# Key-query products of a delta-rule scan by row halves, with loads two steps ahead

## The chip, the core and the metric

The kernel runs on one core of one Trainium2 chip. The metric is the time of one execution on the device, in microseconds; lower is better. Engines are named as the profile names them: PE multiplies matrices (PEld is its loading of the stationary operand), DVE, ACT and POOL work on vectors, and SP issues most of the transfers.

## What is computed

The reference is a two-layer backbone over 512 latent and 256 context tokens. Layer 1 mixes time with a bidirectional RWKV-7 recurrence, and only its scan is touched here:

```python
def wkv_scan(r, w, kk, bvec, k, v, s0, reverse):
    def step(s, inp):
        r_t, w_t, kk_t, b_t, k_t, v_t = inp
        sk = jnp.einsum('bhvk,bhk->bhv', s, kk_t)
        s = s * w_t[:, :, None, :] - sk[..., None] * b_t[:, :, None, :] + v_t[..., None] * k_t[:, :, None, :]
        return s, jnp.einsum('bhvk,bhk->bhv', s, r_t)
```

The delta rule is the term with `sk`: each token takes from the state what the state says under its key `kk_t`. The scan runs over the context first, then over the latent tokens, once forwards and once backwards, for 16 heads of 64 columns.

## The kernel before

The scan works on chunks of 64 tokens. `order` (line 1049) pairs a forward chunk with a backward one: 4 steps over the context, then 8 over the latent tokens, 12 in all. A step handles both directions `d` and, for each of 8 values of `kt`, two heads `n`. On the 128 partitions, direction 0 has its keys and queries in rows 64 to 127 and direction 1 in rows 0 to 63 (`half(1 - d)`).

Two functions share the work. `tm_step(i, kt)` carries the recurrence of step `i` for one pair of heads: products into the PSUM tile `sc` (line 47 is the helper that issues every matmul), with ACT, DVE and POOL between them. `tm_feed(i + 1)` is a generator that prepares the next step; `tm_scan` advances it once after each `kt` of step `i`. It issues the loads of the keys (`KB`, line 1067), queries (`QZ`, line 1068) and values (`W`, line 1071), then forms the products of keys and queries in four groups `g`, masks them into `G` (DVE, line 1082), copies the raw queries into half of `G` (ACT, line 1089), and transposes the keys (line 1096).

The product of one head is one matmul for both directions:

```python
x = 2 * m * (2 * j + n)
self.mm(ps[:, x:x + 2 * m], KB[g // 2][:, 2 * (g % 2) + j, n], QZ[:, 2 * g + j, n, :, 0:m], True, True)
```

The stationary operand is `KB`, 128 rows by 128 columns. `QZ` holds the two directions side by side, and the rows of the other direction are zeros, set once by POOL (line 1289). A context step has `m` = 64 (the delta rule's queries alone), a latent step `m` = 128 (these, and the output's queries behind them). In fp32 every matmul appears in the profile as two passes, each with a load of its stationary operand. `tm_step` reads the output's queries from `QZ` too, for the product `sc<-S,QZ`.

The buffers decide when a load may start: `KB` has 2 buffers, both of one step; `QZ` has 2, one for each step; `W` has 2. So the keys of the next step wait for the transposes of this feed, and its queries for the last read of the step before.

The order on each engine is not the order of the code: a scheduler with a timing model sets it when the program is built, and each engine then runs its list strictly in order. Transfers are SP's list. `tm_invert` and `tm_below` (the inverses of the triangular blocks) and `tm_post` (normalisation of finished chunks) run in between, on DVE, POOL, ACT and PE.

Of the kernel before, what the change touches and what calls it, by code (L numbers as in the profile page):

```python
# [7 lines left out]
F32 = mybir.dt.float32  # L8
F32R = mybir.dt.float32r
I32 = mybir.dt.int32  # L10
AF = mybir.ActivationFunctionType
# [4 lines left out]
P = 128  # L16
D = 1024
KT = 8
# [16 lines left out]
class Net:  # L35
# [908 lines left out]
    def tm_prep(self, kt, lw):  # L944
# [49 lines left out]
        for d in range(2):  # L994
# [4 lines left out]
            else:  # L999
                (nc.vector if kt == KT - 1 else nc.gpsimd).tensor_mul(X[:, 1], X[:, 1], k)  # L1000
                ek, eq, er = E[1][:, :, 0:64], E[0][:, :, 1:65], E[0][:, :, 0:64]
            nc.gpsimd.tensor_copy(self.dec0[:, kt, d], E[1][:, :, 64])
            KB = self.sb([P, 12, 128], F32, "KB", 3)
            nc.vector.tensor_mul(KB.rearrange("p c (b i) -> p b c i", b=2), X.rearrange("p b (c i) -> p b c i", i=64),
                                 ek.unsqueeze(1).to_broadcast([P, 2, 12, 64]))
            nc.sync.dma_start(self.kbd[d, kt], KB)
            ql, qc = self.sb([P, 8, 128], F32, "ql", 3), self.sb([P, 4, 64], F32, "qc", 3)
# [41 lines left out]
    order = [(c, 19 - c) for c in range(8, 12)] + [(c, 7 - c) for c in range(8)]  # L1049
    half = staticmethod(lambda n: slice(64 * n, 64 * n + 64))  # L1050

    def tm_feed(self, i, KB=None, W=None):

        nc, half = self.nc, self.half
        f = self.feeds[i] = {}
        cs = self.order[i]
        lat = cs[0] < 8
        m = 128 if lat else 64
        KB = KB or [self.sb([P, 4, 2, 128], F32, "KB", 2) for _ in range(2)]
        W = f["W"] = W or self.sb([P, KT, 2, 2, 64], F32, "W", 2)  # L1060
        QZ = f["QZ"] = self.QZ[i % 2]
        by = lambda z: z.rearrange("k (n p) m -> p (k n) m", n=2)
        flat = lambda z: z.rearrange("p k n m -> p (k n) m")
        for d in range(2):
            h = half(1 - d)
            for g in range(2):
                nc.sync.dma_start(flat(KB[g][h]), by(self.kbd[d, 4 * g:4 * g + 4, :, cs[d]]))
            nc.sync.dma_start(flat(QZ[h, :, :, d, 0:m]), by(self.qld[d, :, :, cs[d]] if lat else self.qcd[d, :, :, cs[d] - 8]))
        for d in range(2):
            v = self.vd[64 * cs[d]:64 * cs[d] + 64].rearrange("t (k n v) -> t k n v", n=2, v=64)  # L1070
            nc.sync.dma_start(W[half(d), :, d], v)
        f["G"], f["KT"] = [], []
        yield
        for g in range(4):
            ps = self.mm2()
            for j in range(2):
                for n in range(2):
                    x = 2 * m * (2 * j + n)
                    self.mm(ps[:, x:x + 2 * m], KB[g // 2][:, 2 * (g % 2) + j, n], QZ[:, 2 * g + j, n, :, 0:m], True, True)
            G = self.sb([P, 2, 2, 2, m], F32, "G", 8)  # L1080
            f["G"].append(G)
            nc.vector.tensor_mul(G.rearrange("p k n d t -> p (k n) d t"),  # L1082
                                 ps[:, :8 * m].rearrange("p (k d t) -> p k d t", d=2, t=m),
                                 self.gmask[:, :, 0:m].unsqueeze(1).to_broadcast([P, 4, 2, m]))
            if i:

                for d in range(2):
                    h = half(1 - d)
                    nc.scalar.activation(G[h, :, :, d, 0:64], QZ[h, 2 * g:2 * g + 2, :, d, 0:64], AF.Copy)
            yield  # L1090
        for g in range(2):
            ps = self.mm2()
            for j in range(4):
                for n in range(2):
                    x = 256 * j + 128 * n
                    nc.tensor.transpose(ps[:, x:x + 128], KB[g][:, j, n], self.ident)  # L1096
            T = self.sb([P, 4, 2, 128], F32, "KT", 3, pool=self.gp)
            nc.scalar.activation(T, ps.rearrange("p (k n x) -> p k n x", k=4, n=2), AF.Copy)
            f["KT"].append(T)
            yield  # L1100
# [58 lines left out]
    def tm_step(self, i, kt):  # L1159

        nc, half, order = self.nc, self.half, self.order
        f, cs = self.feeds[i], order[i]
        lat, first, last = cs[0] < 8, i == 0, i == len(order) - 1
        g, j = kt // 4, kt % 4
        W = f["W"][:, kt]
        XT = self.XT[i // 2][:, i % 2]
        Q = f["QZ"][:, kt]
        G = f["G"][kt // 2][:, kt % 2]
        K = f["KT"][g][:, j]
        S, Sd = self.S[g], self.Sd[g]  # L1170
        units = [(d, n) for n in range(2) for d in range(2)]
        pr = self.ps([P, 512], "sc", 4, pool=self.sps)
        col = lambda b, d: slice(128 * b + 64 * d, 128 * b + 64 * d + 64)
        for d, n in units:
            h = half(d) if first else slice(0, P)
            self.mm(pr[half(1 - d), col(0, n)], G[h, n, d, 0:64], W[h, d, n], True, True)
        rh = self.sb([P, 2, 64], F32, "rh", 4, pool=self.gp)
        nc.scalar.activation(rh, pr[:, 0:128].rearrange("p (n v) -> p n v", n=2), AF.Copy)
        for d, n in units:
            h = half(1 - d)  # L1180
            self.mm(pr[h, col(1, n)], XT[h, n, kt], rh[h, n], True, True)
        nc.vector.copy_predicated(W, self.umask.unsqueeze(2).unsqueeze(3).to_broadcast([P, 2, 2, 64]),
                                  pr[:, 128:256].rearrange("p (n v) -> p n v", n=2).unsqueeze(1).to_broadcast([P, 2, 2, 64]))
        if not last:
            for d, n in units:
                self.mm(pr[half(1 - d), col(2, n)], K[:, n, half(1 - d)], W[:, d, n], True, True)
            if j == 0:
                self.S2 = self.sb([P, 4, 2, 64], F32, "S", 4, pool=self.gp)
            for n in range(2):
                m = self.dec[:, n, kt, i:i + 1]  # L1190
                if first:
                    nc.vector.tensor_scalar(self.S2[:, j, n], pr[:, col(2, n)], m, None, op0=OP.mult)
                else:
                    nc.vector.scalar_tensor_tensor(self.S2[:, j, n], pr[:, col(2, n)], m, Sd[:, j, n],  # L1194
                                                   op0=OP.mult, op1=OP.add)
            if j == 3:
                W2 = self.feeds[i + 1]["W"]
                for d in range(2):
                    h = half(1 - d)
                    nc.scalar.activation(W2[h, 4 * g:4 * g + 4, d], self.S2[h], AF.Copy)  # L1200
            if j == 3 and i < len(order) - 2:
                m = self.dec[:, :, 4 * g:4 * g + 4, i + 1].rearrange("p n k -> p k n")
                self.Sd[g] = self.sb([P, 4, 2, 64], F32, "Sd", 3, pool=self.gp)
                nc.gpsimd.tensor_mul(self.Sd[g], self.S2, m.unsqueeze(3).to_broadcast([P, 4, 2, 64]))
        if lat:
            units = [(d, n) for d in range(2) for n in range(2)]
            for d, n in units:
                self.mm(pr[half(n), col(3, d)], G[:, n, d, 64:128], W[:, d, n], d == 0, False)
            for d, n in units:
                self.mm(pr[half(n), col(3, d)], Q[:, n, d, 64:128], S[:, j, n], False, d == 1)  # L1210
            lo, hi = min(cs), max(cs)
            Y = self.Y[:, kt, lo:hi + 1:hi - lo]
            o = pr[:, 384:512].rearrange("p (d v) -> p d v", d=2)
            if cs[0] < cs[1]:
                nc.scalar.activation(Y, o, AF.Copy)
            else:
                nc.vector.tensor_add(Y, Y, o[:, ::-1])
        if j == 3 and not last:
            self.S[g] = self.S2
# [56 lines left out]
    def tm_scan(self):  # L1276
        nc, a, half = self.nc, self.a, self.half
# [1 line left out]
        nc.sync.dma_start(self.gmask, a["gmask"])  # L1279
        self.umask = self.sb([P, 2], I32, "umask")  # L1280
        nc.sync.dma_start(self.umask, a["umask"])

        qz = lambda j: self.sb([P, KT, 2, 2, 128], F32, "QZ%d" % j)
        q = qz(0)
        ahead = [self.sb([P, 4, 2, 128], F32, "KB", 2) for _ in range(2)], self.sb([P, KT, 2, 2, 64], F32, "W", 2)
        self.QZ = [q, qz(1)]
        for j, z in enumerate(self.QZ):
            for d in range(2):
                nc.gpsimd.memset(z[half(d), :, :, d], 0.0)  # L1289
        self.feeds, self.S, self.Sd = {}, [None, None], [None, None]  # L1290
        n, below = len(self.order), iter(())
        for _ in self.tm_feed(0, *ahead):
            pass
        for i in range(n):
            feed = self.tm_feed(i + 1) if i + 1 < n else iter(())
            for kt in range(KT):
                self.tm_step(i, kt)
# [230 lines left out]
```

## Time and profile before

| | |
|---|---|
| median of 3 runs | 2260.74 us (2259.57 to 2262.29) |
| the profiled execution | 2269.31 us, 0.38% over the median |
| its span | 2267.5 us |
| PE busy in the span | 2023.4 us (89%) |
| DVE, ACT, POOL busy | 1145.4, 869.6, 519.6 us |
| mean granted clock of PE | 0.942 |
| the scan, by its first and last product | about 1464 to 1815 us of the span |

The span is the time from the first to the last instruction of the profiled execution. PEclk is the granted share of PE's full clock of 2.4 GHz; 0.5 is 1.2 GHz. A busy share is an average over stages: outside the scan PE is busy nearly all of the time, inside it is not.

### The profile page before, as it was taken

To read this page: it belongs to the slowest core of one execution; us is meant where nothing else is said; L and a number is where in the kernel's file an instruction comes from. 1 tells how busy PE (TensorE), PEld (TensorE's weight loads), DVE (VectorE), ACT (ScalarE), POOL (GpSimd) and SP (SyncE) were. 2 spreads that over 40 slices of the span, in tenths; PEclk is the share of its full clock that TensorE was granted. 3 is DMA by queue.
4 is the path that set the end of the run, shared out by engine and by line. 5 is a ranking of instruction groups with operands and counts; after the bars stand their busy time and mean duration, and the time that the engine had idled before them with its cause. 6 is when DMAs were issued, how large, how long until landed. Compare 5 with 4: busy or idle time off the path is not lost. (4 is left out here: it accounts for less than half of the span.)

```text
span 2267.5 us, 37320 instructions
## 1 busy us (share of the span) xinstructions
PE 2023.4 (89%) x15710; PEld 1619.3 (71%) x15710; DVE 1145.4 (51%) x1835; ACT 869.6 (38%) x1333; POOL 519.6 (23%) x530
## 2 busy tenths in 40 slices
PE   5888889999999999997987769779787778999999
PEld 3666547778888888875765449667676666888887
DVE  4556664342222222328647997648575684333333
ACT  3664454231121221317744543346454432232321
POOL 0122331010010100105004983661500220110110
PEclk8999999999999999998998778889898999999999
DMA  7324441123333122212224659396644440222222
GB/s 282 119 86 136 143 164 41 37 94 119 124 129 113 56 64 67 98 42 79 93 88 148 236 223 214 71 143 102 113 91 80 76 140 19 93 93 93 93 93 93
DMA packets 231944, 248.93 MB, mean 110 GB/s; under 512 B 52448, under 2 KB 209504, under 8 KB 225376
## 3 DMA queue, kind: packets, MB, share of 16 engines
q1 hardware_dynamic: 229728, 241.30, 36.8%
q0 software_dynamic: 896, 3.15, 0.4%
q8 instruction: 123, 2.02, 0.4%
q10 hardware_dynamic: 1152, 2.10, 0.2%
q14 instruction: 45, 0.37, 0.1%
HBM read 200.82 MB, written 41.94 MB: 107 GB/s over the span
## 5 line engine op out<-in xcount | busy, mean ns | idle before, releaser
L264 ACT ACTIVATE whi<-wst 128x1024 fp32r<-128x1024 f32 x160 | 169.2, 1059 | 587.3 <-PE mm L47 567.0
L47 PE MATMUL mm<-hhi,whi 128*128 128x512 f32 (+1 forms) x992 | 346.8, 356 | 16.2 <-ACT hhi L250 6.7
L47 PE MATMUL mm<-hlo,whi 128*128 128x512 f32 (+1 forms) x992 | 352.0, 356 | 3.6 <-DVE hlo L251 3.4
L47 PE MATMUL mm<-hhi,wlo 128*128 128x512 f32 (+1 forms) x992 | 349.6, 353 | 0.0
L265 DVE TENSOR_TENSOR wlo<-wst,whi 128x1024 fp32r<-128x1024 f32 x160 | 199.9, 1251 | 255.2 <-ACT whi L264 252.4
L345 POOL TENSOR_TENSOR mp<-mr 128x768 f32<-128x768 f32 (+1 forms) x64 | 109.9, 1719 | 848.1 <-ACT mr L344 848.1
L47 PE MATMUL mm<-ahi,wlo 128*128 128x512 f32 (+1 forms) x704 | 252.9, 359 | 0.0
L47 PE MATMUL mm<-ahi,whi 128*128 128x512 f32 (+1 forms) x704 | 252.9, 360 | 0.0
L47 PE MATMUL mm<-alo,whi 128*128 128x512 f32 (+1 forms) x704 | 252.5, 359 | 0.0
L300 DVE SCALAR_TENSOR_TENSOR Xt<-mm,mod,Xt 128x512 f32<-128x512 f32 (+1 forms) x112 | 70.6, 653 | 336.8 <-PE mm L47 336.6
L47 PEld LDWEIGHTS mm<-hhi,whi 128*128 128x128 f32 x992 | 187.8, 191 | 55.2 <-ACT hhi L250 8.7
L47 PEld LDWEIGHTS mm<-hlo,whi 128*128 128x128 f32 x992 | 188.9, 190 | 32.1 <-DVE hlo L251 6.6
L47 PEld LDWEIGHTS mm<-hhi,wlo 128*128 128x128 f32 x992 | 188.4, 190 | 28.3 <-issue 0.8
L47 PEld LDWEIGHTS mm<-ahi,whi 128*128 128x128 f32 x704 | 132.2, 188 | 28.1 <-issue 6.7
L47 PEld LDWEIGHTS mm<-ahi,wlo 128*128 128x128 f32 x704 | 132.5, 188 | 22.0 <-DVE wlo L265 1.1
L47 PEld LDWEIGHTS mm<-alo,whi 128*128 128x128 f32 x704 | 132.4, 188 | 21.9
L47 PE MATMUL mm<-QZ,KB 128*128 128x256 f32 (+1 forms) x384 | 96.4, 408 | 48.1 <-DMA QZ<-qlr 20.3
L47 PEld LDWEIGHTS mm<-QZ,KB 128*128 128x128 f32 x384 | 74.1, 227 | 60.3 <-issue 26.3
L347 DVE TENSOR_TENSOR alo<-mp,ahi 128x768 fp32r<-128x768 f32 (+1 forms) x64 | 54.9, 858 | 113.1 <-ACT ahi L346 113.0
L1082 DVE TENSOR_TENSOR G<-mm,gmask 128x1024 f32<-128x1024 f32 (+1 forms) x48 | 50.2, 1047 | 88.1 <-PE mm L47 87.8
L346 ACT ACTIVATE ahi<-mp 128x768 fp32r<-128x768 f32 (+1 forms) x64 | 47.3, 739 | 110.3 <-POOL mp L345 110.3
L47 PE MATMUL sc<-W,G 128*64 128x64 f32 (+1 forms) x1280 | 67.8, 233 | 12.8 <-DVE S L1194 10.3
(462 smaller groups left out, 4207.7 us busy)
## 6 DMA issues: line engine op xcount, KB each, us to landing
wst<-in_mlp_w_dram SPq DMA_DIRECT2D x64, 1024.0 KB, 5.4
wst<-in_ada_w_dram SPq DMA_DIRECT2D x48, 1024.0 KB, 6.4
kbr<-KB SPq DMA_DIRECT2D x16, 768.0 KB, 4.5
KB<-kbr SPq DMA_DIRECT2D x48, 256.0 KB, 5.6
wst<-in_rw_w_rkv_dram SPq DMA_DIRECT2D x8, 1024.0 KB, 5.4
qlr<-ql SPq DMA_DIRECT2D x16, 512.0 KB, 3.3
QZ<-qlr SPq DMA_DIRECT2D x16, 512.0 KB, 8.8
wst<-in_hy_w_in_dram SPq DMA_DIRECT2D x7, 1024.0 KB, 5.3
```

The source lines that it names most:

```text
L47: self.nc.tensor.matmul(out, lhsT, rhs, start=start, stop=stop)
L264: nc.scalar.activation(hi, w, AF.Copy)
L265: nc.vector.tensor_sub(lo, w, hi.bitcast(F32))
L300: self.nc.vector.scalar_tensor_tensor(x, ps[:, c0:c1], self.m(l, chunk, v, kt), x, op0=OP.mult, op1=OP.add)
L345: nc.gpsimd.tensor_mul(p[:, :n], r[:, :n], r[:, :n])
L346: nc.scalar.activation(h[:, :n], p[:, :n], AF.Copy)
L347: nc.vector.tensor_sub(o[:, :n], p[:, :n], h[:, :n].bitcast(F32))
L1082: nc.vector.tensor_mul(G.rearrange("p k n d t -> p (k n) d t"), ps[:, :8 * m].rearrange("p (k d t) -> p k d t", d=2, t=m), self.gmask[:, : ...
```

## The change

The loads leave `tm_feed` for a new function, `tm_load(i, late)`. Its early part loads the keys (now 4 buffers, two steps) and the delta rule's queries as a tile `Q` of their own without zeros (3 buffers). Its late part loads the output's queries into `R` (2 buffers, with zeros in the other direction's rows, set by POOL) for latent steps, and the values. At the start of step `i`, `tm_scan` issues the late part of step `i + 1` and the early part of step `i + 2`.

The product of one head becomes two matmuls for a context step and four for a latent one, each with 64 rows, 128 stationary columns and 64 moving columns; direction 0 writes to the first PSUM bank of the tile and direction 1 to the second. The mask reads the two banks with one instruction of the same size as before. `G` has 7 buffers in place of 8. In bytes of SBUF a partition the buffers come to the same sum.

```diff
--- before.py
+++ after.py
@@ -1049,44 +1049,65 @@
     order = [(c, 19 - c) for c in range(8, 12)] + [(c, 7 - c) for c in range(8)]
     half = staticmethod(lambda n: slice(64 * n, 64 * n + 64))
 
-    def tm_feed(self, i, KB=None, W=None):
+    def tm_load(self, i, late):
+
 
         nc, half = self.nc, self.half
-        f = self.feeds[i] = {}
+        f = self.feeds.setdefault(i, {})
         cs = self.order[i]
         lat = cs[0] < 8
-        m = 128 if lat else 64
-        KB = KB or [self.sb([P, 4, 2, 128], F32, "KB", 2) for _ in range(2)]
-        W = f["W"] = W or self.sb([P, KT, 2, 2, 64], F32, "W", 2)
-        QZ = f["QZ"] = self.QZ[i % 2]
         by = lambda z: z.rearrange("k (n p) m -> p (k n) m", n=2)
         flat = lambda z: z.rearrange("p k n m -> p (k n) m")
+        if late:
+            W = f["W"] = self.sb([P, KT, 2, 2, 64], F32, "W", 2)
+            R = f["R"] = self.R[i % 2]
+            for d in range(2):
+                if lat:
+                    h = half(1 - d)
+                    nc.sync.dma_start(flat(R[h, :, :, d]), by(self.qld[d, :, :, cs[d], 64:128]))
+            for d in range(2):
+                v = self.vd[64 * cs[d]:64 * cs[d] + 64].rearrange("t (k n v) -> t k n v", n=2, v=64)
+                nc.sync.dma_start(W[half(d), :, d], v)
+            return
+        KB = f["KB"] = [self.sb([P, 4, 2, 128], F32, "KB", 4) for _ in range(2)]
+        Q = f["Q"] = self.sb([P, KT, 2, 64], F32, "Q", 3)
         for d in range(2):
             h = half(1 - d)
+            nc.sync.dma_start(flat(Q[h]), by(self.qld[d, :, :, cs[d], 0:64] if lat else self.qcd[d, :, :, cs[d] - 8]))
             for g in range(2):
                 nc.sync.dma_start(flat(KB[g][h]), by(self.kbd[d, 4 * g:4 * g + 4, :, cs[d]]))
-            nc.sync.dma_start(flat(QZ[h, :, :, d, 0:m]), by(self.qld[d, :, :, cs[d]] if lat else self.qcd[d, :, :, cs[d] - 8]))
-        for d in range(2):
-            v = self.vd[64 * cs[d]:64 * cs[d] + 64].rearrange("t (k n v) -> t k n v", n=2, v=64)
-            nc.sync.dma_start(W[half(d), :, d], v)
+
+    def tm_feed(self, i):
+
+        nc, half = self.nc, self.half
+        f = self.feeds[i]
+        lat = self.order[i][0] < 8
+        m = 128 if lat else 64
+        KB, Q, R = f["KB"], f["Q"], f["R"]
         f["G"], f["KT"] = [], []
         yield
         for g in range(4):
+
             ps = self.mm2()
             for j in range(2):
                 for n in range(2):
-                    x = 2 * m * (2 * j + n)
-                    self.mm(ps[:, x:x + 2 * m], KB[g // 2][:, 2 * (g % 2) + j, n], QZ[:, 2 * g + j, n, :, 0:m], True, True)
-            G = self.sb([P, 2, 2, 2, m], F32, "G", 8)
+                    for d in range(2):
+                        x, h, k = 512 * d + m * (2 * j + n), half(1 - d), KB[g // 2]
+                        self.mm(ps[:, x:x + 64], k[h, 2 * (g % 2) + j, n], Q[h, 2 * g + j, n], True, True)
+                    for d in range(2):
+                        x, h, k = 512 * d + m * (2 * j + n), half(1 - d), KB[g // 2]
+                        if lat:
+                            self.mm(ps[:, x + 64:x + 128], k[h, 2 * (g % 2) + j, n], R[h, 2 * g + j, n, d], True, True)
+            G = self.sb([P, 2, 2, 2, m], F32, "G", 7)
             f["G"].append(G)
             nc.vector.tensor_mul(G.rearrange("p k n d t -> p (k n) d t"),
-                                 ps[:, :8 * m].rearrange("p (k d t) -> p k d t", d=2, t=m),
+                                 ps.rearrange("p (d x) -> p d x", d=2)[:, :, :4 * m].rearrange("p d (k t) -> p k d t", t=m),
                                  self.gmask[:, :, 0:m].unsqueeze(1).to_broadcast([P, 4, 2, m]))
             if i:
 
                 for d in range(2):
                     h = half(1 - d)
-                    nc.scalar.activation(G[h, :, :, d, 0:64], QZ[h, 2 * g:2 * g + 2, :, d, 0:64], AF.Copy)
+                    nc.scalar.activation(G[h, :, :, d, 0:64], Q[h, 2 * g:2 * g + 2], AF.Copy)
             yield
         for g in range(2):
             ps = self.mm2()
@@ -1164,7 +1185,7 @@
         g, j = kt // 4, kt % 4
         W = f["W"][:, kt]
         XT = self.XT[i // 2][:, i % 2]
-        Q = f["QZ"][:, kt]
+        R = f["R"][:, kt]
         G = f["G"][kt // 2][:, kt % 2]
         K = f["KT"][g][:, j]
         S, Sd = self.S[g], self.Sd[g]
@@ -1207,7 +1228,7 @@
             for d, n in units:
                 self.mm(pr[half(n), col(3, d)], G[:, n, d, 64:128], W[:, d, n], d == 0, False)
             for d, n in units:
-                self.mm(pr[half(n), col(3, d)], Q[:, n, d, 64:128], S[:, j, n], False, d == 1)
+                self.mm(pr[half(n), col(3, d)], R[:, n, d], S[:, j, n], False, d == 1)
             lo, hi = min(cs), max(cs)
             Y = self.Y[:, kt, lo:hi + 1:hi - lo]
             o = pr[:, 384:512].rearrange("p (d v) -> p d v", d=2)
@@ -1279,19 +1300,21 @@
         nc.sync.dma_start(self.gmask, a["gmask"])
         self.umask = self.sb([P, 2], I32, "umask")
         nc.sync.dma_start(self.umask, a["umask"])
-
-        qz = lambda j: self.sb([P, KT, 2, 2, 128], F32, "QZ%d" % j)
-        q = qz(0)
-        ahead = [self.sb([P, 4, 2, 128], F32, "KB", 2) for _ in range(2)], self.sb([P, KT, 2, 2, 64], F32, "W", 2)
-        self.QZ = [q, qz(1)]
-        for j, z in enumerate(self.QZ):
-            for d in range(2):
-                nc.gpsimd.memset(z[half(d), :, :, d], 0.0)
         self.feeds, self.S, self.Sd = {}, [None, None], [None, None]
         n, below = len(self.order), iter(())
-        for _ in self.tm_feed(0, *ahead):
+        self.R = [self.sb([P, KT, 2, 2, 64], F32, "R%d" % j) for j in range(2)]
+        for r in self.R:
+            for d in range(2):
+                nc.gpsimd.memset(r[half(d), :, :, d], 0.0)
+        for i, late in ((0, False), (0, True), (1, False)):
+            self.tm_load(i, late)
+        for _ in self.tm_feed(0):
             pass
         for i in range(n):
+            if i + 1 < n:
+                self.tm_load(i + 1, True)
+            if i + 2 < n:
+                self.tm_load(i + 2, False)
             feed = self.tm_feed(i + 1) if i + 1 < n else iter(())
             for kt in range(KT):
                 self.tm_step(i, kt)
```

**SP's list in a late latent step.** Names: `KB` keys, `W` values, `QZ`, `Q` and `R` queries; XT<-in_rw_w_o is a weight of a later stage. Before:

```order
L1067 DMA KB<-kbr 64x8x128 x4
L1359 DMA XT<-in_rw_w_o_dram 128x8x256
L1071 DMA W<-vdr 64x8x128
L1068 DMA QZ_11365<-qlr 64x16x128 x2
L1071 DMA W<-vdr 64x8x128
L1067 DMA KB<-kbr 64x8x128 x4
```

and now:

```order
L1070 DMA W<-vdr 64x8x128
L1067 DMA R_11361<-qlr 64x16x64 x2
L1070 DMA W<-vdr 64x8x128
L1076 DMA Q<-qlr 64x16x64 x2
L1078 DMA KB<-kbr 64x8x128 x4
L1382 DMA XT<-in_rw_w_o_dram 128x8x256
L1070 DMA W<-vdr 64x8x128
L1067 DMA R_11362<-qlr 64x16x64 x2
```

Before, the four loads of keys stand in front of the queries that the same feed needs; now the two loads of `R` stand behind one load of values only, and the keys and `Q` that follow are those of the step after.

**PE's list around the first products of a latent feed.** Names: `sc` is the recurrence of the running step, `mm_` with a number is the PSUM tile of one group of products, the numbers behind `QZ` and `R` tell their two buffers apart, and 64x64 or 128x256 is the size of an output. Before, with the last read of the old `QZ_11361` just above the first row:

```order
L47 MATMUL sc<-W,KT 64x64 x4
L47 MATMUL sc<-rh,XT 64x64 x4
L47 MATMUL sc<-W,G 64x64 x4
L47 MATMUL sc<-S,QZ_11365 64x64 x4
L47 MATMUL sc<-W,G 64x64 x8
L47 MATMUL sc<-S,QZ_11365 64x64 x4
L47 MATMUL sc<-rh,XT 64x64 x4
L47 MATMUL sc<-W,KT 64x64 x4
L47 MATMUL sc<-W,G 64x64 x8
L47 MATMUL sc<-W,KT 64x64 x4
L47 MATMUL sc<-rh,XT 64x64 x8
L47 MATMUL mm_14767<-QZ_11361,KB 128x256 x4
```

and now:

```order
L47 MATMUL sc<-S,R_11362 64x64 x4
L47 MATMUL sc<-W,G 64x64 x12
L47 MATMUL sc<-S,R_11361 64x64 x4
L47 MATMUL sc<-W,G 64x64 x4
L47 MATMUL sc<-rh,XT 64x64 x8
L47 MATMUL sc<-W,G 64x64 x4
L47 MATMUL sc<-rh,XT 64x64 x4
L47 MATMUL sc<-W,KT 64x64 x8
L47 MATMUL sc<-rh,XT 64x64 x4
L47 MATMUL mm_14732<-R_11362,KB 128x64
L47 MATMUL mm_14780<-R_11362,KB 128x64
L47 MATMUL sc<-W,KT 64x64 x4
```

Before, the first products of the feed stand together (4 here, and the next group's 4 right behind) after 56 matmuls of the recurrence since the last read of the old `QZ`; now the products with `Q` are already out, those with `R` follow 48 matmuls after the last read of the old `R`, and they stand in short pieces between those of the recurrence.

## Rows read from the trace of the kernel before

**Rows 1.** Chain of waits from 1400 to 1840 us, its sum by line and releaser.
```profile
by line: PE mm L47 21.4%; PE sc L47 13.1%; DMA QZ<-qlr 9.2%; issue 7.3%; DMA KB<-kbr 6.0%; DVE zt L1124 4.1%; DVE Z L1125 4.0%; PE mm L1096 3.9%; DMA XT<-ldr 3.6%; DVE G L1082 2.4%; POOL Z L1125 1.8%; POOL QZ L1289 1.6%; POOL zt L1124 1.6%;
```

**Rows 2.** Stretches between products of keys and queries: length, busy time by engine, PEclk, DMA share.
```profile
core 0: us, PE busy (x) PEld busy (x) DVE busy (x) ACT busy (x) POOL busy (x), PEclk, DMA share, GB/s
...
1568.30:1608.60 40.30, 33.17 (x641) 27.30 (x640) 34.09 (x80) 20.86 (x48) 21.08 (x36) 0.94 0.59 103
...
1677.90:1714.00 36.10, 28.89 (x545) 24.30 (x545) 24.36 (x73) 15.62 (x35) 3.17 (x3) 0.88 0.55 104
```

**Rows 3.** Waits of PE from 1464.8 to 1815 us: us in total, times, longest us.
```profile
PE mm L47 <- DMA QZ<-qlr: 20.3, 4, 7.8
...
PE mm L47 <- issue: 11.6, 2, 8.1
...
PE mm L47 <- POOL Z L1125: 8.3, 1, 8.3
...
PE mm L47 <- DMA KB<-kbr: 6.8, 4, 2.8
```

**Rows 4.** Waits of SP's queue in the same stretch.
```profile
SPq L1067 <- PE sc L47: 94.2, 15, 23.7
```

**Rows 5.** SP's issues from 1691 to 1739 us: start us, us, line, transfer, count.
```profile
1691.26 2.89 SPq L1067 DMA_DIRECT2D KB<-kbr  x4
...
1696.76 4.08 SPq L1068 DMA_DIRECT2D QZ<-qlr  x2
```

**Rows 6.** Chain of waits again, in order of time: start us, us, what.
```profile
1604.77 6.39 PE mm L47 x16
...
1674.11 5.86 PE mm L47 x16
...
1697.97 12.19 DMA QZ<-qlr
...
1710.21 6.59 PE mm L47 x16
...
1743.28 5.43 PE mm L47 x16
...
1767.64 9.39 DMA KB<-kbr
...
1778.28 3.75 PE mm L47 x8
```

**Rows 7.** Instructions on tile QZ: duration ns min/median/max, first and last start, forms.
```profile
L47 PEld LDWEIGHTS sc<-S,QZ x512: 132/138/227, 1576.5 to 1816.2; 128*64 128x64 f32 x171
...
L47 PE MATMUL sc<-S,QZ x512: 222/222/314, 1576.6 to 1816.2; 128*64 128x64 f32 x171
...
L47 PEld LDWEIGHTS mm<-QZ,KB x384: 186/190/338, 1463.6 to 1794.7; 128*128 128x128 f32 x192
...
L47 PE MATMUL mm<-QZ,KB x384: 271/379/796, 1463.8 to 1794.9; 128*128 128x256 f32 x128, 128*128 128x128 f32 x64
```

**Rows 8.** Timeline of PE, a pass and three bursts: start us, us, instructions, count.
```profile
1324.51 0.19 PE L47 MATMUL mm<-ones,bon 64*64 64x1 f32 x1
...
1324.57 0.90 PE L47 MATMUL mm<-ones,bon 64*64 64x1 f32 x26
...
1751.00 0.58 PE L47 MATMUL sc<-W,KT 128*64 128x64 f32 x14
...
1756.97 1.99 PE L47 MATMUL mm<-QZ,KB 128*128 128x256 f32 x8
```

**Rows 9.** Timeline of PE, three groups of eight passes in a row.
```profile
1695.27 0.45 PE L47 MATMUL sc<-rh,XT 64*64 64x64 f32 x8
1695.65 0.45 PE L47 MATMUL sc<-W,G 128*64 128x64 f32 x8
1695.93 0.40 PE L47 MATMUL sc<-S,QZ 128*64 128x64 f32 x8
```

**Rows 10.** DMA queues from 1568 to 1782 us: packets, MB, share of 16 engines.
```profile
q1 hardware_dynamic: 44736, 21.38, 56.8%
```

## The prediction

> **What bounds the kernel now.** The page gives a PE that is busy 89% of the span, but that is a mean over stages; the change lives in the scan, about 1464 to 1815 us. I first read the chain of waits there by its sum [rows 1]: matmuls lead it, but 9.2% of those 440 us are loads of `QZ` and 6.0% loads of `KB`. Then the stretches between the first products of one feed and the next [rows 2]: a latent step takes some 36 to 40 us, PE is busy for 29 to 33 of them, PEclk is 0.94 and 0.88, and the DMA queues are only 55 to 59% busy. So neither PE nor the queues are full: something makes them take turns.
>
> The waits of PE say what [rows 3]. Eleven waits before products of keys and queries add up to 20.3 + 11.6 + 8.3 + 6.8 = 47.0 us. Two groups are named after loads. The "issue" and the POOL one I read as loads too: a wait is put down to the last event that the profile shows, and each of these stands before the first product of a feed, in the midst of a burst of loads. SP's queue says why the loads are late [rows 4]: the issues of keys alone waited 94.2 us for PE to free the old keys. One step shows it [rows 5]: four loads of keys at 1691.26 us, `QZ` only at 1696.76, and the second `QZ` lands 12.19 us after its issue at 1697.97, right when PE starts at 1710.21 [rows 6].
>
> The waits cost twice. After each long one PE runs at half of its clock (1.2 GHz). The first 16 passes over 256 columns took 6.39, 5.86, 6.59 and 5.43 us [rows 6]; at full clock 8 take 1.99 [rows 8], so 16 take 3.98. That is 2.4 + 1.9 + 2.6 + 1.5 us lost, and by the same comparison 1.8 at 1778.28 (8 passes in 3.75): 10.2 us in these five; shorter ones I leave out.
>
> **The change, part by part.**
>
> *Loads.* Keys and `Q` now come two steps ahead, so no feed should wait for them. What can still be late is `R`: it is released where `QZ` was, by the last read two steps back. In SP's new list only one load of values (512 packets) stands before the two of `R` (1024 each): 2560 packets, where `QZ` had four loads of keys (2048), one of values (512) and itself (2048), 4608. From the queues' row [rows 10] a packet takes 214 us x 16 x 0.568 / 44736 = 43 ns of one of 16 engines; 4608 of them need 12.4 us, close to the 12.19 seen, and 2560 need 6.9. So `R` lands some 5 us sooner, behind about as much work of PE (48 matmuls against 56 in the lists). The six or so long waits of 3.5 to 8 us each keep 0 to 3; I leave 8 us of the 47.0, a gain of **39**. With them most of the clock loss goes: I take **9** of 10.2.
>
> *Products.* Before there are 384 passes [rows 7]. At full clock a 256-column pass costs (1.99 - 0.38) / 7 = 0.23 us, the 0.38 being the length of one pass [rows 7, 8], so the 256 latent ones cost 59 us; the 128 context ones, half as long, 15: 74 us. Now there are 640 matmuls, 1280 passes over 64 columns with a stationary operand of 64 rows by 128 columns. No row shows that form, so I bound it.
> - Low end: two column halves that alternate run 14 passes in 0.58 us, one lasting 0.22 [rows 7, 8], that is (0.58 - 0.22) / 13 = 28 ns a pass, the moving of 64 columns shared by two. If row halves share as well and the load hides, 1280 x 28 ns = 36 us, 38 less than now.
> - The load bounds it: passes with a single moving column and a load of 64 columns still go at (0.90 - 0.19) / 25 = 28 ns, on two tiles in turn [rows 8]. So a load of 64 columns takes 57 ns of its tile, however little follows it. A load of 128 columns lasts 52 ns more (190 against 138) [rows 7], so 109 ns. With two row halves side by side a pass costs 54.5 ns, 1280 of them 70 us: 4 less than now.
> - High end: the halves load one after the other. 1280 x 109 ns = 140 us, 66 more.
>
> I take the middle, **4** less: the single-column row is nearest to it, since there two tiles in different rows and columns do load side by side. The Trainium skill speaks against a larger gain (TensorE: Matmul & The Clock Gate, section LDWEIGHTS (loading the stationary operand)): the time of a load goes by its columns, about columns / 1.2 ns, and not by its rows, so half as many rows save nothing. The trace agrees with its 107 ns for 128 columns (109 here); an estimate by the page alone puts the products at 68 us side by side and 137 in series, close to those from rows.
>
> *Changes of form.* PE's list now has 395 stretches of one form in the scan, before 281 (my count in both lists), because the products stand in short pieces. From a group of eight passes to one of another form it is 0.38 us, to one of the same form 0.28 [rows 9]. 114 x 0.10 = 11 us more, all counted as on the path, though some will fall into waits.
>
> *Costed at nothing.* A latent step moves as many bytes in 2048 more packets, 5.5 us of the queues at 43 ns; the loads two steps ahead hide it in the 43% that is idle [rows 10]; without that cover it is up to 44 us over 8 steps. SP issues two more loads a latent step, before anything waits for them. DVE's mask and ACT's copies keep their sizes; fewer zeros are set on POOL; the eighth `G` buffer would be needed only when the running step has already freed one.
>
> *Sum.* -39 - 9 - 4 + 11 = **-41 us**: the profiled execution would go from 2269.3 to 2228, and the median, 0.38% lower, from 2260.7 to **2220 us**. Behind the loads, DVE and the chain through ACT and DVE are next in line; DVE is 34 of 40 us busy in one stretch [rows 2], so I do not count on more.
>
> **The rivals.**
> 1. *Row halves run at 28 ns.* The products give 38 us instead of 4: 2220 - 34 = 2186 us. For it: column halves do just that [rows 8]. Against it: the load of 128 columns [rows 7]. The Trainium skill would have it so (TensorEngine Tiling (Array Packing), section Theoretical Speedup): a contraction of 64 or less gives up to twice the speed.
> 2. *`R` takes the place of `QZ`.* It has the same release point, and if the new bursts are as long as the old, every wait for `QZ` stays. Then only the waits for keys go: the 6.8, the 8.3 that is put down to POOL, and the 8.1 under "issue" [rows 3], which is the one at 1778.28 behind a load of `KB` [rows 6]. That is 23 us, with 2 of clock: -23 - 2 - 4 + 11 = -18, 2243 us. This is also the case in which the change does not load ahead as it says, because SP's list waits at `W` and `R` with the keys behind them. For it: SP runs strictly in order. Against: all those loads are for a step later.
> 3. *Slower: the two row halves load in series.* 66 us more instead of 4 less: -41 + 70 = +29, 2290 us. It decides from 54.5 + 41 / 1.28 = 87 ns a pass on (41 us over 1280 passes). For it: no row shows two row halves with the same columns. Against: tiles with different rows and columns do not wait for each other [rows 8].
>
> **How the numbers follow.** Forecast 0.50, rival 1 0.18, rival 2 0.17, rival 3 0.12, and 0.03 for a mixture of slower products and shorter waits that lands at no change. The forecast's own range is 2204 to 2236 (the remaining wait 0 to 15 us, the changes of form 0 to 17, the clock 5 to 10). To hold 8 in 10 I reach to rival 1 below and rival 2 above: **2182 to 2250 us**; only rival 3 and no change lie outside. No change is within 0.2% (4.5 us), about what a measurement of this kernel tells apart. Faster 0.85, same 0.03, slower 0.12.
>
> **What would show it.** Right: the waits of PE before the products shrink from 47 us to under 15; no transfer of keys or `Q` is in the chain; the products of `Q` and `R` are some 55 ns apart; PEclk in the latent steps is over 0.95; a latent step takes about 30 us. Rival 1 shows as 28 ns, rival 3 as 109 ns between passes; rival 2 as waits of 5 to 8 us for `R`. I am wrong outright if a stretch is as long as before with fewer waits: then DVE or the chain of one head was the bound behind the loads.

## The result, and the profile after

| | before | changed |
|---|---|---|
| median of 4 runs each, on one chip | 2261.51 us (2259.57 to 2263.85) | 2377.28 us (2372.92 to 2379.53) |
| ratio, with its 95% interval | | 1.0515 (1.0502 to 1.0528) |
| profiled execution, its span | 2269.31, 2267.5 us | 2376.36, 2374.6 us |
| mean granted clock of PE | 0.942 | 0.902 |

The change is slower by 116 us; 2220 was forecast. The scan takes nearly all of it: from 1464 us its last product is now 456.7 us away, in place of 352.5. The ratios here and below leave out three executions that lie far from the others of the same kernel (5326.30 us in run 2, 2316.66 and 2372.47 us in before), and so does the time of run 2. The whole scan of each kernel in the view of stretches, first of before, then of the changed kernel with four stretches inside it (columns as in [rows 2]: length, busy time of PE, PEld, DVE, ACT, POOL with their instructions, PEclk, DMA share, GB/s):

```profile
1464.00:1816.50 352.50, 284.95 (x5248) 241.88 (x5246) 218.29 (x545) 171.11 (x366) 106.14 (x152) 0.89 0.60 103
```

```profile
1464.00:1920.70 456.70, 378.48 (x6137) 336.83 (x6135) 219.56 (x544) 170.28 (x366) 96.97 (x147) 0.70 0.47 81
...
1576.70:1580.10 3.40, 3.40 (x66) 3.06 (x66) 3.30 (x11) 1.32 (x3) 0.94 (x1) 1.00 0.42 93
...
1586.90:1600.60 13.70, 13.70 (x177) 12.28 (x175) 4.20 (x9) 5.37 (x12) 1.06 (x1) 0.50 0.00 1
1600.60:1604.00 3.40, 3.40 (x29) 2.85 (x27) 0.00 (x0) 2.35 (x6) 0.00 (x0) 0.50 0.93 158
1604.00:1610.80 6.80, 6.80 (x112) 5.75 (x111) 2.92 (x10) 2.19 (x4) 0.90 (x1) 1.00 1.03 197
```

Read the PEclk column against PE's busy time. Over the scan the clock fell from 0.89 to 0.70. It has two levels; the stretches of the scan at 1.2 GHz alone (PEclk 0.50) are ten in before and fourteen in the changed kernel. The longest of each, and the sum of all of each, before first:

```profile
1774.08:1784.32 10.24, 6.04 (x52) 4.88 (x54) 1.71 (x3) 0.83 (x2) 1.93 (x1) 0.50 0.71 120
sum 75.07, PE 51.82 PEld 43.79 DVE 23.59 ACT 14.45 POOL 17.06; mean PE 5.18 PEld 4.38 DVE 2.36 ACT 1.44 POOL 1.71
```

```profile
1491.34:1532.30 40.96, 30.57 (x384) 26.21 (x386) 9.22 (x26) 12.56 (x27) 14.03 (x23) 0.50 0.77 121
...
sum 269.65, PE 229.94 PEld 207.55 DVE 118.33 ACT 96.68 POOL 59.52; mean PE 16.42 PEld 14.82 DVE 8.45 ACT 6.91 POOL 4.25
```

So 270 us of the scan are at 1.2 GHz in place of 75, and PE is busy for 230 of them in place of 52. A busy microsecond at half clock does half a microsecond's work; by that estimate 115 us are lost in place of 26: **89 us of the 116 have this form.** PE need not idle for it: from 1586.90 to 1600.60 it is busy for all of 13.70 us, and the clock is 0.50 throughout.

PE's timeline in the changed kernel says what it does there, and what a pass costs (start us, us, instructions, count):

```profile
1587.01 0.64 PE L47 MATMUL mm<-R,KB 64*128 64x64 f32 x4
1587.43 0.64 PE L47 MATMUL mm<-Q,KB 64*128 64x64 f32 x4
1587.86 0.64 PE L47 MATMUL mm<-R,KB 64*128 64x64 f32 x4
1588.29 0.64 PE L47 MATMUL mm<-Q,KB 64*128 64x64 f32 x4
...
1600.56 1.97 PE L1117 MATMUL mm<-ident,KB 128*128 128x128 f32 x8
...
1762.57 0.39 PE L47 MATMUL mm<-R,KB 64*128 64x64 f32 x4
1762.79 0.39 PE L47 MATMUL mm<-Q,KB 64*128 64x64 f32 x4
...
1763.91 0.39 PE L47 MATMUL mm<-R,KB 64*128 64x64 f32 x4
```

At full clock, from 1762.57 to 1763.91, 24 passes start in 1.34 us: 56 ns a pass. That is the price that was forecast (54.5). From 1587.01 to 1588.29, at half clock, it is 12 in 1.28 us: 107 ns. The row halves work side by side, as hoped; they do so at half speed. At the end of this stretch stand eight transposes of 128 by 128, from 1600.56, and passes of `sc` behind them; from 1604.00 on the clock is 1.00.

The waits of PE (1464 to 1920.7 us; us in total, times, longest) that answer to [rows 3], and those that grew:

```profile
PE sc L47 <- DVE W L1203: 17.5, 9, 6.2
PE mm L47 <- DMA R<-qlr: 15.1, 6, 6.0
PE mm L47 <- DMA KB<-kbr: 14.4, 3, 13.4
PE mm L47 <- DVE G L1103: 10.1, 4, 3.3
PE sc L47 <- DVE S L1215: 7.1, 1, 7.1
```

Waits for loads are 29.5 us, from 47.0. One of them is 13.4 us, for the keys of the third context step, and SP's queue (timeline from 1480 to 1502 us) shows why: SP issues without a pause, and four loads of `R` for latent steps (the first product with `R` starts at 1574.6), eight of `bo` for another part of the program and two of `Q` stand ahead of these keys in its list, so that they start only at 1495.42.

```profile
1480.64 6.16 SPq L1067 DMA_DIRECT2D R<-qlr  x4
1487.03 5.56 SPq L1254 DMA_DIRECT2D bo<-vdr  x7
...
1495.42 2.87 SPq L1078 DMA_DIRECT2D KB<-kbr  x4
```

The same waits for DVE before (1464 to 1815 us); together they grew from 14.4 to 34.7 us:

```profile
PE sc L47 <- DVE S L1194: 10.3, 7, 4.5
...
PE sc L47 <- DVE W L1182: 2.5, 4, 1.0
PE mm L47 <- DVE G L1082: 1.6, 3, 1.0
```

### The profile page after: what moved, and what is told of

It reads as the page before. It is cut to its first block, busy times and chain, and to the rows that moved or that the text cites. A ratio compares the mean times of both kernels' runs of the same rounds, so it can differ in the third digit from the quotient of the medians.

```text
span 2374.6 us, 39091 instructions
## 1 busy us (share of the span) xinstructions
PE 2125.9 (90%) x16606; PEld 1724.3 (73%) x16606; DVE 1150.0 (48%) x1835; ACT 869.5 (37%) x1333; POOL 514.6 (22%) x530
## 5 line engine op out<-in xcount | busy, mean ns | idle before, releaser
L47 PE MATMUL mm<-Q,KB 64*128 64x64 f32 x768 | 111.5, 358 | 20.5 <-DMA KB<-kbr 14.4
L47 PEld LDWEIGHTS mm<-Q,KB 64*128 64x128 f32 x768 | 93.1, 258 | 27.6 <-issue 15.1
L47 PE MATMUL mm<-R,KB 64*128 64x64 f32 x512 | 84.6, 363 | 15.1 <-DMA R<-qlr 15.1
L47 PE MATMUL sc<-W,G 128*64 128x64 f32 (+1 forms) x1280 | 83.0, 266 | 9.4 <-DVE S L1215 7.1
```

The lines of the kernel that those rows point to most:

```text
L47: self.nc.tensor.matmul(out, lhsT, rhs, start=start, stop=stop)
```

## The experiments

Theory 1 was formed on this profile: the row halves bring the clock down, and everything PE does in the scan pays. Theory 2: the loss is in the order of loads, the waits for `R` and the fewer buffers. The first four runs take the change apart. Times are medians; each ratio is to before on the same chip, with its 95% interval; the clock is that of the stretch from 1464 us to the scan's end.

| run | what it is | us | ratio | clock |
|---|---|---|---|---|
| 1 | before, row halves with 64 columns | 2401.20 | 1.0592 (1.0541 to 1.0642) | 0.66 |
| 2 | before, row halves, 128 columns in latent passes | 2327.99 | 1.0287 (1.0250 to 1.0323) | 0.73 |
| 3 | changed kernel, passes filled up to 128 columns | 2318.71 | 1.0244 (1.0215 to 1.0273) | 0.81 |
| 4 | before, keys two steps ahead | 2266.37 | 1.0015 (1.0000 to 1.0030) | 0.91 |
| 5 | run 4, feed one head later | 2258.41 | 0.9974 (0.9960 to 0.9988) | 0.90 |
| 6 | before, row halves in latent products alone, 128 columns | 2269.47 | 1.0029 (1.0014 to 1.0043) | 0.82 |
| 7 | before, six buffers of `G` | 2266.39 | 1.0006 (0.9996 to 1.0016) | 0.89 |
| 8 | changed kernel, whole rows | **2241.02** | 0.9899 (0.9879 to 0.9919) | 0.92 |
| 9 | run 8, `R` two steps ahead too | **2239.22** | 0.9894 (0.9874 to 0.9914) | 0.92 |
| 10 | run 8, passes of 64 columns | 2384.85 | 1.0554 (1.0508 to 1.0599) | 0.77 |

### Run 1: the row halves alone

```diff
-                    x = 2 * m * (2 * j + n)
-                    self.mm(ps[:, x:x + 2 * m], KB[g // 2][:, ...], QZ[:, 2 * g + j, n, :, 0:m], True, True)
+                    for t in range(0, m, 64):
+                        for d in range(2):
+                            x, h = 512 * d + m * (2 * j + n) + t, half(1 - d)
+                            self.mm(ps[:, x:x + 64], KB[g // 2][h, ...], QZ[h, 2 * g + j, n, d, t:t + 64], True, True)
```

> The kernel before with one part of the change alone: the products by row halves, 64 moving columns in a pass, loads and zeros as before. Theory 1 (the short row-half passes bring TensorE's granted clock down to its lower level, 1.2 GHz, and all its work in the scan then runs at half speed): 80 to 130 us slower than before, 2340 to 2390 us, with the granted clock at 0.5 for over half of the stretch from 1464 us to the scan's end. Theory 2 (the passes are well priced at 55 ns; the loss comes from the new order of loads, the waits for R and fewer buffers of G): within 20 us of before, since none of those is in this kernel, and the clock as before.

Measured 2401.20 us, 5.9% slower, the clock 0.66. Theory 1 has its direction and a little more than its size; theory 2 falls, as none of its causes is in this kernel. The products by themselves cost more than the whole change, so the rest of the change gains.

### Run 2: row halves, 128 columns

```diff
+                    for d in range(2):
+                        x, h = 512 * d + m * (2 * j + n), half(1 - d)
+                        self.mm(ps[:, x:x + m], KB[g // 2][h, ...], QZ[h, 2 * g + j, n, d, 0:m], True, True)
```

> The kernel before with the products by row halves, but with 128 moving columns in a latent pass (a head's queries of both kinds side by side, as they lie in QZ): 512 latent passes in place of 1024. Loads as before. Theory 1: a pass takes the same 55 ns, its load being what bounds it, but moves twice the columns, so the clock stays up: the latent products take 28 us in place of 59, 15 to 45 us faster than before, 2215 to 2245 us, granted clock over 0.85 in the latent steps. Rival to it (half the rows alone bring the clock down, whatever the columns): as slow as the run with 64 columns or nearly, over 2300 us. Theory 2 (order of loads and buffers): as theory 1, so this run alone says nothing for or against it.

A miss: 65 us slower by the ratio where a gain was expected. Half of the loss of run 1 is gone with half of the latent passes, but the clock is still 0.73. The expectation had overlooked that a context step has only 64 queries a direction, so `m` is 64 there and the context passes are those of run 1.

### Run 3: more work in each pass

```diff
+            for jn in (3, 2, 1, 0):
...
+                        self.mm(ps[:, x:x + 128], k[h, ...], R[h, 2 * g + j, n, d].unsqueeze(1).to_broadcast([64, 2, 64]), True, True)
...
+                        self.mm(ps[:, x - 64:x + 64], k[h, ...], q.unsqueeze(1).to_broadcast([64, 2, 64]), True, True)
```

> The changed kernel, with every pass of the row halves (but the first of Q of each group) moved over 128 columns in place of 64: the same 64 columns twice, the second copy being overwritten by the next product. As many loads, passes and transfers as in the changed kernel, twice the columns moved, no result changed. Theory 1: the clock comes back for much of the scan, so it is 60 to 130 us faster than the changed kernel (2245 to 2315 us) although it does more. Theory 2: no faster than the changed kernel, 2375 us or more.

2318.71 us: 59 us less than the changed kernel (61 by the ratios), 4 us above theory 1's range, at a clock of 0.81 in place of 0.70. This is the plainest evidence against "less work is faster": the same passes and loads, in another order within a group, nearly twice the columns, all of the added ones useless, and a shorter time.

### Run 4: keys two steps ahead, alone

```diff
+        KB = f["KB"] = [self.sb([P, 4, 2, 128], F32, "KB", 4) for _ in range(2)]
...
+            self.tm_load(i + 1, True)
+            self.tm_load(i + 2, False)
...
-            G = self.sb([P, 2, 2, 2, m], F32, "G", 8)
+            G = self.sb([P, 2, 2, 2, m], F32, "G", 6)
```

> The other part of the change alone: keys two steps ahead, queries with values, as in the changed kernel's list of loads, products over full rows with zeros as before; six buffers of G in place of the changed kernel's seven, for space. Theory 1: the prediction's term for the loads holds, 20 to 48 us faster than before (2213 to 2241 us), granted clock over 0.9 in the latent steps. Theory 2 (the new order of loads or the buffers of G cause the loss): 50 to 120 us slower than before.

Neither: no measurable difference. Keys are out of PE's waits, but `QZ` is as late as ever. The waits of PE in run 4 (1464 to 1810 us), SP's issue of one `QZ`, and the first product behind it in PE's timeline:

```profile
PE mm L47 <- issue: 15.9, 3, 6.6
PE sc L47 <- DVE W L1194: 11.1, 7, 3.9
PE mm L47 <- DMA QZ<-qlr: 10.7, 3, 6.0
PE mm L47 <- POOL Z L1137: 9.6, 1, 9.6
```

```profile
1667.86 3.97 SPq L1066 DMA_DIRECT2D QZ<-qlr  x2
```

```profile
1680.74 1.62 PE L47 MATMUL mm<-QZ,KB 128*128 128x256 f32 x3 [5.96 <-DMA QZ<-qlr]
```

The two `QZ` loads start at 1667.86, when the step two back has done its last read, and the product starts 12.9 us later. With the "issue" and POOL waits read as loads, as in the prediction (the one put down to POOL ends 0.14 us after a `QZ` of the context has landed), waits for `QZ` alone are 36.2 us, where those for `QZ` and keys together were 47.0; waits for DVE's `W` grew to 11.1 us from 2.5. So the wait for `QZ` took over most of what loading keys early took away. That was the rival of the prediction in which `R` takes the place of `QZ`; here it is `QZ` itself.

### Runs 5 to 7: later products, latent halves alone, fewer buffers

Run 5 adds a bare `yield` ahead of the feed's first product.

> The run with the loads ahead (products as before, six buffers of G), with the feed's products, masks and turns all moved one head later in each step, so that the late queries have some 4 us more to land. If the release point of QZ is what kept the loads ahead from paying: the waits of 3 to 6.6 us before the latent products shrink to 0 to 2 us, with them the stretches at half clock behind them: 15 to 45 us faster than before, 2216 to 2246 us. Rival (what PE waited for there is given back at the next wait, for DVE's products of the step): within 10 us of before.

2258.41 us, 0.26% under before. The time is the rival's, but not its reason: the five longest waits before latent products did not shrink, they are still 3.1 to 6.4 us. What was moved back in the feed gave `QZ` no more work of PE to land behind: in the longest of them named after `QZ`, 5.2 us from its issue to the start of the wait, where run 4 has 6.9.

Run 6 is run 2 with the context products as in before.

> The kernel before with row halves for the latent products alone, 128 moving columns in a pass; the context products over whole rows with zeros, all loads as before. Theory 1a (only passes with 64 moving columns lower the clock): the clock stays as before and the latent products take 30 us less: 15 to 35 us faster than before, 2226 to 2246 us. Theory 1b (the clock follows the share of the array that works, so the zeros that are left out had kept it up): the granted clock in the latent steps is lower than before, 0.75 to 0.87, and the 30 us are given back: 2250 to 2300 us.

2269.47 us: theory 1b by its ranges. The clock in the scan is 0.82 (before 0.89), and leaving out half of the latent products' multiplications, all of them with zeros, brings nothing. With busy time at half clock counted half, PE's work in the scan fell from 259 to 230 us, the 30 us of the expectation; but PE is now busy at half clock for 94 us in place of 52, which gives 21 of them back. From run 6 to run 2 only the context products go to row halves with 64 columns: the ratio rises by 0.0258, 58 us, for work that took 15 us by the prediction's count. The profiles put it in the context steps: the first `sc<-S,QZ`, in the first latent step, starts at 1622.8 us in run 2 and at 1567.1 in run 6.

Run 7 has six buffers of `G` in place of eight and nothing else.

> The kernel before with six buffers of G in place of eight, nothing else. Control for the runs with six or seven: within 8 us of before if the buffers don't matter; if the loads ahead did gain and the buffers gave it back, 20 to 45 us slower than before.

No difference, so the buffers of runs 4, 5 and 8 cost nothing that can be measured.

### Run 8: whole rows again, the loads of the change kept

```diff
-                    for d in range(2):
-                        x, h, k = 512 * d + m * (2 * j + n), half(1 - d), KB[g // 2]
-                        self.mm(ps[:, x:x + 64], k[h, 2 * (g % 2) + j, n], Q[h, 2 * g + j, n], True, True)
...
+            for z, o in ((Q, 0), (R, 512))[:2 if lat else 1]:
+                for j in range(2):
+                    for n in range(2):
+                        x = o + 128 * (2 * j + n)
+                        self.mm(ps[:, x:x + 128], KB[g // 2][:, ...], z[:, 2 * g + j, n], True, True)
```

> The changed kernel with the row halves alone undone: Q and R split and loaded as in it, keys two steps ahead, but Q too with its zeros, and each product over whole rows with 128 moving columns (Q's passes of a group first, then R's); DVE's mask in two halves, Q in two buffers, six of G. Theory 1 (the row halves cost the clock): all of the loss goes, 2215 to 2262 us, granted clock over 0.85 in the scan. Theory 2 (split loads, their order and the short transfers of R cost it): 2330 us or more. For the term of the loads: if R, half as long as QZ and needed later, lands in time, 20 to 45 us faster than before.

2241.02 us, 1.0% faster than before and 6% faster than the changed kernel. The zeros are back, and so is the clock, 0.92. The scan of run 8 in the view of stretches, and PE's waits for loads (1464 to 1790 us) with the new wait in line:

```profile
1464.00:1790.00 326.00, 287.71 (x5504) 255.68 (x5504) 221.31 (x579) 171.29 (x366) 98.64 (x148) 0.92 0.70 116
```

```profile
PE sc L47 <- DVE W L1200: 12.0, 5, 3.8
PE mm L47 <- DMA KB<-kbr: 8.6, 2, 5.2
PE mm L47 <- DMA R<-qlr: 7.1, 3, 3.7
...
PE mm L47 <- issue: 2.7, 1, 2.7
```

Loads cost 8.6 + 7.1 + 2.7 = 18.4 us in place of 47.0. `R` is half as long as `QZ` was and, with `Q`'s passes of a group first, needed a little later: its longest wait is 3.7 us, `QZ`'s was 7.8 [rows 3]. Waits for DVE's `W` are longer (12.0 against 2.5), but those for its `S` are gone (0.4 against 10.3), so what the loads won is not taken back by waits: PE idles for 36.8 us of the scan in place of 67.6. About 8 us go into PE's own work, 267 us at full clock in place of 259.

### Run 9: `R` two steps ahead as well

```diff
-            R = f["R"] = self.R[i % 2]
+        Q, R = f["Q"], f["R"] = self.Q[i % 2], self.R[i % 3]
...
-        KB = f["KB"] = [self.sb([P, 4, 2, 128], F32, "KB", 4) for _ in range(2)]
+        KB = f["KB"] = [self.sb([P, 4, 2, 128], F32, "KB", 3) for _ in range(2)]
```

> The run before this one with R in three buffers, loaded two steps ahead in front of the keys (for space, keys in three tiles and G in five buffers): no load of the scan then waits for the end of the running step but the values. If loads that land late are what PE waits for at the latent products: waits for R and Q under 5 us in all, 20 to 55 us faster than before, 2208 to 2243 us. Rival (PE meets the next wait in their place, for the running step's DVE or for keys): 2245 to 2270 us.

2239.22 us: the lowest time of all, but not told apart from run 8. It lies in the first range, near its end (24 us under before by the ratio), and no wait is put down to `R` or `Q` any more. What the rival said is there too: PE meets the next wait in their place, 15.5 us for keys, in the context steps, where run 8 waited 8.6 (the view of waits, 1464 to 1790 us):

```profile
PE mm L47 <- DMA KB<-kbr: 15.5, 4, 8.4
PE sc L47 <- DVE S L1211: 4.9, 3, 2.0
```

### Run 10: whole rows, 64 columns

```diff
-                        self.mm(ps[:, x:x + 128], KB[g // 2][:, ...], z[:, 2 * g + j, n], True, True)
+                        for d in range(2):
+                            self.mm(ps[:, x + 64 * d:x + 64 * d + 64], KB[g // 2][:, ...], z[:, 2 * g + j, n, d], True, True)
```

> The run with whole rows (loads of the changed kernel), with each pass over 128 columns split in two over 64: 1280 passes, each with its load of 128 columns over all rows, where there were 640. No row halves at all. At 112 ns a pass, the spacing of that run, the products take 143 us in place of 72: 71 us more if the clock stays. Rival to theory 1 (it is the half rows as such, two tiles side by side, that cost the clock): 2300 to 2325 us, granted clock in the scan about 0.9. Theory 1, by the share of the array that works (here too half of what the 128-column passes keep at work, since the load takes as long): the clock falls as in the changed kernel, to 0.65 to 0.78 in the scan, and 2370 to 2450 us.

2384.85 us at a clock of 0.77: theory 1; the half rows as such are not needed for the loss. Three stretches of run 10 in a row, and a piece of its timeline:

```profile
1710.40:1720.60 10.20, 7.53 (x159) 6.64 (x154) 3.82 (x9) 2.58 (x9) 0.36 (x1) 1.00 1.25 169
1720.60:1754.80 34.20, 34.10 (x344) 32.62 (x345) 21.14 (x48) 12.58 (x27) 1.06 (x1) 0.50 0.16 26
1754.80:1806.00 51.20, 45.09 (x826) 41.38 (x827) 27.90 (x84) 20.39 (x47) 3.17 (x3) 1.00 0.65 123
```

```profile
1723.02 4.53 PE L47 MATMUL mm<-R,KB 128*128 128x64 f32 x20
```

This is the row to remember. For 34.20 us PE is busy for 34.10 and its clock is 0.50; in the next 51.20 it idles for 6.1 and the clock is 1.00. Work with the keys, nearly all of it passes that load 128 columns for each 64 moved, is 104 of the 344 passes in the slow stretch and fills 23.09 us of it. But 190 such passes run in the next stretch at 1.00, so the form of the passes alone does not set the level. The Trainium skill (TensorE: Matmul & The Clock Gate, section HAM oscillation — how this bites in real kernels) ties a lost clock to idle gaps between bursts of matmuls. Waits of 3.5 to 8 us do stand ahead of the slow products of before, as the prediction read them; this row disagrees: two waits ahead of it (PE idles for 2.7 us of the 10.20 before) may have let the clock fall, but no gap holds it down for the 34 us after. So it is with all six stretches at half clock of this scan: PE idles for 0.9 to 4.5 us of the 7.0 us ahead of each, and is then busy for 204 of their 215 us.

Its size comes out of its parts too. From run 8 the passes go from 640 to 1280 at 112 ns, 71 us; PE is busy at half clock for 204 us of the scan against 41 in run 8, half of the difference is 81. Together 152 us; by the ratios it is (1.0554 - 0.9899) x 2263 = 148.

## Why the prediction was wrong

- **The clock, the step that failed.** The prediction priced every pass at full clock and said of half clock: "The waits cost twice", and "With them most of the clock loss goes: I take 9 of 10.2". So half clock was taken as something that waits cause and that shorter waits heal. Idle time does stand ahead of it (run 10); but the runs showed that it then stays with PE busy, and that the share of the scan that it takes differs with the form of the products: with whole rows and 128 columns the scan has 0.92 (run 8), with whole rows and 64 columns 0.77 (run 10), with half rows side by side and 128 columns for most 0.81 (run 3), with half rows and 64 columns 0.70 (the changed kernel). In place of 9 us gained, the clock took 89 more. The prediction's loss in before was too small as well: PE is busy at half clock for 52 us of that scan, a loss of 26 us, of which the five bursts hold 10.2.
- **Loads, -39 (and -9 for the clock behind them).** Right in direction, too large. Runs 8 and before differ by 22 us. PE's waits for loads shrank by 28.6 us there, not by 39, because `R` (7.1) and the keys of the context (8.6) still come late, and 8 us of PE's own work came on top. In the changed kernel itself they shrank by 17.5. And the prediction credited the whole to loading ahead. Run 4 shows that keys ahead alone bring nothing; run 8, with `QZ` split, its late half shorter and `Q`'s passes first, does gain. Rival 2 (`R` takes the place of `QZ`) was half right: in the changed kernel PE still waits 15.1 us for `R`, where it was 20.3 for `QZ` [rows 3].
- **Products, -4.** The price held: 56 ns a pass at full clock, 54.5 forecast. The load of 128 columns bounds the pass (over whole rows it takes 112 ns with 128 columns moved in run 8 and with 64 in run 10), and the halves load side by side. Rival 1 (28 ns) and the mechanism of rival 3 (in series, 109 ns) are both out; that a pass takes 107 ns in the slow stretches is the clock, seen in the PEclk of the same stretch.
- **Changes of form, +11.** No run measured it by itself. Together with the products it was to be +7; PE's work in the scan, counted at full clock, grew by 4.5 us.
- **Costed at nothing.** No run takes the shorter packets and the added loads apart; the DMA share in the scan is 0.47, from 0.60. Not counted was that loads of `R` and `bo` stand ahead of keys in SP's list: 13.4 us in one step.
- **The sign.** "Slower" stood at 0.12, for the halves in series. The kernel is slower by another mechanism that was on no list.

The scan from 1464 us to its last product, in us, taken apart by the views of stretches. Busy time at half clock is counted half lost and half work, which is an estimate:

| | length | PE idle | lost at half clock | PE's work at full clock |
|---|---|---|---|---|
| before | 352.5 | 67.6 | 25.9 | 259.0 |
| changed | 456.7 | 78.2 | 115.0 | 263.5 |
| run 3 | 403.4 | 74.3 | 62.3 | 266.8 |
| run 6 | 345.9 | 69.3 | 47.0 | 229.6 |
| run 8 | 324.5 | 36.8 | 20.4 | 267.3 |
| run 10 | 464.0 | 30.4 | 101.8 | 331.8 |

From before to the changed kernel that is 89.1 us at half clock, 10.6 of idle time and 4.5 of work: 104.2 of the 116, and the two profiled spans differ by 107. In the idle time, waits for loads fell by 17.5 us and those for DVE's `W`, `S` and `G` grew by 20.3, which fits a chain that runs between DVE and a slower PE; that it is the cause is argued, no run shows it alone. The row halves as a whole are measured: run 1 against before is +5.9%, the changed kernel against run 8 is (1.0515 - 0.9899) = +6.2%, so they cost about the same with either set of loads.

Open is what exactly the clock goes by: the runs show which forms go with how much half clock, not why it stays. Runs 3 and 8 move nearly the same columns in the products, and run 8 is still 78 us faster; by the table 42 of that is the clock, 37 idle time, and none PE's own work.

## What to carry to other kernels

Price TensorE work at the clock that it will be granted, not only in time at full clock: in run 10 passes that load 128 columns to move 64 stood in a stretch that was busy without a gap and yet ran at 1.2 GHz, and all other work between them paid as well. A saving of zeros in a matmul can be worth nothing: in the changed kernel the load of the stationary operand bounds the pass, and in run 6 the 30 us that were saved went back, most of them through the clock. Where a change has two parts, time each alone: here one part was worth 1% and the other cost 6%.

## What was not expected of the hardware

- PE busy for 34.10 us of 34.20 at a granted clock of 0.50 (run 10).
- A kernel with nearly twice the moving columns and not one useful result more is 59 us faster (run 3 against the changed kernel).
- Leaving out half of the latent products' multiplications, all with zeros, took the scan's clock from 0.89 to 0.82 and gained nothing (run 6).
- The longest stretch at half clock is 10.24 us in before and 40.96 us in the changed kernel. In run 10 such stretches start behind idle time (0.9 to 4.5 us of the 7.0 us ahead) and go on with PE busy.
